# Twenty weight blocks whose low parts come from ScalarE and an adding DMA instead of a VectorE subtraction

## The chip, the core and the metric

The kernel runs on one core of a Trainium2 chip. The core has a matrix engine (TensorE, in the profile PE, with its weight loads as PEld), a vector engine (VectorE, DVE), a scalar engine (ScalarE, ACT), a general engine (GpSimd, POOL) and a queue engine (SyncE, SP) that here issues the DMAs. Each engine works through its own list of instructions in order; semaphores tie the lists together. Sixteen DMA engines move data between DRAM and the on-chip memory SBUF; PSUM holds what TensorE sums.

The metric is the time of one execution in microseconds (us), the median of several. The profile is one execution recorded by the hardware, whose own time stands beside its span.

## The reference

One layer of a bidirectional hybrid encoder on a sequence of 512 tokens, 1024 features, all in float32:

```python
h = rms_norm(x, g[0])
proj = h @ w_in[l]
hy_u, na_qkv, sc_u, gate_pre = jnp.split(proj, splits, axis=-1)
kf = hyena_filters(L, ...)                  # long filters, by a small sine network
y_a = hyena_mixer(hy_u, hy_short_w[l], kf, hy_bias[l])   # two long convolutions, by FFT
y_b = neighbourhood_attention(q, k, v, na_rpb[l])
y_c = short_conv_mixer(b_gate, c_gate, x_in, sc_conv_w[l])
merged = gates[:, :, 0] * (y_a @ w_branch[l, 0]) + ...   # three gated branches
x = x + rms_norm(merged @ w_out[l], g[1])
x = x + rms_norm(memory_cross_attention(...), g[3])
x = x + rms_norm(conv_glu_ffn(...), g[5])
```

The change lies in `h @ w_in`, for 20 of the column blocks of `w_in`: those of the Hyena branch that are not projected earlier (8) and those of the short convolution (12).

## The kernel before

**Split products.** TensorE reads float32 numbers here in a rounded form (F32R). To keep precision, each operand is split into a high part `h`, the rounded value, and a low part `l`, the rest, and `mm3` (L84) adds three products: high by high, high by low, low by high. `split` (L80) makes the parts: `high` (L75) is a ScalarE copy with rounding, `low` (L78) a subtraction, on VectorE unless another engine is named. All these helpers record under one line each, so the profile tells them apart by tile: `wh` and `wl` are high and low part of a weight block, `xh` and `xl` those of the normed input.

**Weight blocks.** A block is 128 partitions by 1024 float32 numbers, 512 KB, and is 128 columns of `w_in`. `block` (L92) takes a `wh` and a `wl` tile (four buffers each) and calls `load_split`: `load_raw` (L108) has SP issue a DMA from DRAM into a `wr` tile (three buffers), ScalarE makes `wh` from `wr`, and VectorE makes `wl` as `wr - wh`. A `wr` buffer is free for the next load when VectorE has read it. A `wh` or `wl` buffer is free when TensorE has done the block that used it, four blocks earlier.

**The projection loop.** `projections` (L308) is a generator over the 20 blocks. It asks for two blocks ahead, then for one more each time before it multiplies one: `project` runs 8 steps of `mm3`, 24 matmuls of 512 columns, into one PSUM bank (`mm`).

**What runs around it.** `go` draws blocks from the generator between the steps of the Hyena branch, so the blocks fill TensorE while the other engines work:

- the filter network: `filter_taps` (twice; tiles `hf`, `ha`, `hb`, `la`, `lb`; GpSimd makes `w` and `w3b`), then `spectra` (tiles `od`, `kt`), whose results go out to DRAM (`kd`) on SP and come back as `kst`;
- the wave matrices: `filter_mats` (`cosh`, `cosl`, `sinh`, `sinl`, the low parts on GpSimd) and `hyena_consts` (`wavef`, `wavee`, `waveo`, loaded by SP as `raw<-in_hy_f`, `_e`, `_o`);
- four convolutions: `conv_in` turns the input with TensorE transposes (L490) and splits it into `sh`, `sl`; `conv_forward` multiplies by `wavef` into `aux` banks, copies two of them by ScalarE into `fly` tiles, combines them on VectorE (L523 to L529), and multiplies by the spectrum into two `ab` tiles (L533 to L537). VectorE finishes one of these with four steps (L543 to L546) and GpSimd the other with the same four. `conv_split` makes `ych`, `ysh` (ScalarE) and `ycl`, `ysl` (VectorE), and `conv_back` multiplies them by `wavee`, `waveo` and gates the result (L570);
- `conv3` on the projected blocks (L322, L323; for most of them ScalarE makes `tap` and GpSimd adds it, L329), and the short convolution (`scg`, `scx`, `sct`, `yc`).

**What sets the order.** A scheduling layer places each instruction in its engine's list ahead of time. What a list holds, and so what a waiting instruction holds up behind it, is fixed when the program is built. After the Hyena branch come the neighbourhood attention, the gates, the cross-attention and the gated MLP, in the same manner.

Of the kernel before, what the change touches and what calls it, by code (L numbers as in the profile page):

```python
# [7 lines left out]
F32R = mybir.dt.float32r  # L8
ACT = mybir.ActivationFunctionType
ALU = mybir.AluOpType  # L10
# [3 lines left out]
P = 128  # L14
# [19 lines left out]
def f(ap):  # L34
    return ap.bitcast(F32)
# [15 lines left out]
class Trunk:  # L51
# [40 lines left out]
    def block(self, src):  # L92

        h = self.base.tile([P, 1024], F32R, tag="wh", bufs=4, name="wh")
        lo = self.base.tile([P, 1024], F32R, tag="wl", bufs=4, name="wl")
        self.load_split(h[:], lo[:], src)
        return h, lo

    def block_parts(self, src):
# [208 lines left out]
    def projections(self, srcs, x):  # L308

        srcs = iter(srcs)  # L310
        ws = [self.block(src) for src in islice(srcs, 2)]
        yield
        while ws:
            ws += [self.block(src) for src in islice(srcs, 1)]
            yield self.project(ws.pop(0), x)

    def conv3(self, out, ps, col, spare=False):
# [1030 lines left out]
```

## Time and profile before

| | |
|---|---|
| median of 3 runs | 1112.19 us (1111.86 to 1113.84) |
| the profiled execution, its own time | 1114.05 us |
| its span, first to last instruction | 1112.3 us |
| mean granted TensorE clock | 0.99 of full speed |
| busy over the span | PE 97%, PEld 81%, DVE 63%, ACT 43%, POOL 9% |
| chain of work that ended last | PE 82%, DVE 9%, DMA 3%, ACT 2%, issue 2%, POOL 1% |

The 1.75 us between the profiled execution's time and its span lie outside the instructions. The busy shares are means over stages that differ. The stage of the 20 blocks lies between about 50 and 240 us, and the views in the prediction are read there: the waits of an engine (who waited for whom), groups of instructions by line and shape, the timeline (start, duration, engine, line, operation; at the end the idle time before it and what ended it), and windows (busy time of each engine in a stretch, with the granted clock). Consecutive matmuls overlap in their records: what a matmul costs TensorE is the step from its start to the next one's.

### The profile page before, as it was taken

How to read it: one execution, taken by the hardware profiler on the slowest of the kernel's cores; microseconds unless marked ns; L12 is line 12 of the kernel's file. 1: busy time of each engine (PE TensorE's matmuls, PEld its weight loads, DVE VectorE, ACT ScalarE, POOL GpSimd, SP SyncE). 2: the span in 40 equal slices, each digit the busy share in tenths (PEclk: the TensorE clock that was granted, in tenths of full speed). 3: DMA queues.
4: the chain of work that ended last, by engine and by line, in shares of the span. 5: the costliest groups of instructions: out<-in, count | busy, mean ns of one | idle time of the engine just before them, and what ended most of it. 6: DMA issues, size and time to landing. Idle time of an engine off the chain costs nothing.

```text
span 1112.3 us, 13562 instructions
## 1 busy us (share of the span) xinstructions
PE 1081.6 (97%) x5232; PEld 903.2 (81%) x5232; DVE 696.5 (63%) x1021; ACT 477.3 (43%) x744; POOL 95.4 (9%) x72
## 2 busy tenths in 40 slices
PE   8889989999999999999999999999999999999997
PEld 6668878887888888888789888889888888888886
DVE  6898799985656564344796546576656565642324
ACT  6553532224557453232565444454444444431221
POOL 0161242221121110000000000000000000000000
PEclk9899999999999999999999999999999999999999
DMA  6354723317423312224526421222222222222212
GB/s 218 105 190 161 246 94 107 103 58 167 125 87 100 112 57 95 95 95 160 200 76 205 156 76 57 76 95 95 95 95 95 95 95 97 102 98 101 95 57 75
DMA packets 43532, 125.48 MB, mean 113 GB/s; under 512 B 5097, under 2 KB 11561, under 8 KB 43468
## 3 DMA queue, kind: packets, MB, share of 16 engines
q1 hardware_dynamic: 43468, 124.62, 33.4%
q8 instruction: 41, 0.67, 0.2%
q14 instruction: 23, 0.19, 0.1%
HBM read 115.16 MB, written 7.34 MB: 110 GB/s over the span
## 4 chain that ended last, share of the span: by engine, by line
PE 82%; DVE 9%; DMA 3%; ACT 2%; issue 2%; POOL 1%; SPq 0%; DVEq 0%; ACTq 0%; POOLq 0%
PE mm L88 25%; PE mm L89 25%; PE mm L90 25%; DVE wl L78 2%; PE aux L725 1%; PE aux L89 1%; PE aux L90 1%; PE aux L88 1%; DMA wr<-in_w_in 1%; PE aux L714 1%; ACT wh L75 1%; PE aux L904 1%; DMA raw<-in_hy_o 1%; POOL w L398 0%; DMA wr<-in_w_out 0%
## 5 line engine op out<-in xcount | busy, mean ns | idle before, releaser
L78 DVE TENSOR_TENSOR wl<-wr,wh 128x1024 fp32r<-128x1024 f32 (+1 forms) x171 | 219.8, 1289 | 254.4 <-ACT wh L75 253.6
L75 ACT ACTIVATE wh<-wr 128x1024 fp32r<-128x1024 f32 (+1 forms) x171 | 180.1, 1054 | 308.1 <-PE mm L89 186.7
L89 PE MATMUL mm<-hl,wh 128*128 128x512 f32 (+1 forms) x448 | 167.5, 374 | 0.0
L88 PE MATMUL mm<-hh,wh 128*128 128x512 f32 (+1 forms) x448 | 167.2, 374 | 0.3 <-ACT hh L75 0.3
L90 PE MATMUL mm<-hh,wl 128*128 128x512 f32 (+1 forms) x448 | 167.4, 374 | 0.0
L88 PE MATMUL mm<-xh,wh 128*128 128x512 f32 x416 | 164.6, 396 | 0.0
L89 PE MATMUL mm<-xl,wh 128*128 128x512 f32 x416 | 163.7, 393 | 0.0
L90 PE MATMUL mm<-xh,wl 128*128 128x512 f32 x416 | 163.6, 393 | 0.0
L89 PEld LDWEIGHTS mm<-hl,wh 128*128 128x128 f32 x448 | 84.4, 188 | 15.0 <-DVE hl L78 0.2
L90 PEld LDWEIGHTS mm<-hh,wl 128*128 128x128 f32 x448 | 84.3, 188 | 15.0
L88 PEld LDWEIGHTS mm<-hh,wh 128*128 128x128 f32 x448 | 84.1, 188 | 15.2 <-ACT hh L75 0.5
L90 PEld LDWEIGHTS mm<-xh,wl 128*128 128x128 f32 x416 | 78.9, 190 | 17.1 <-issue 0.3
L88 PEld LDWEIGHTS mm<-xh,wh 128*128 128x128 f32 x416 | 79.0, 190 | 15.8
L89 PEld LDWEIGHTS mm<-xl,wh 128*128 128x128 f32 x416 | 78.9, 190 | 15.7
L88 PE MATMUL mm<-wh,act 128*128 128x512 f32 x176 | 68.5, 389 | 0.0
L89 PE MATMUL mm<-wl,act 128*128 128x512 f32 x176 | 68.5, 389 | 0.0
L90 PE MATMUL mm<-wh,act 128*128 128x512 f32 x176 | 68.3, 389 | 0.0
L88 PEld LDWEIGHTS mm<-wh,act 128*128 128x128 f32 x176 | 33.0, 188 | 7.1 <-issue 0.3
L75 ACT ACTIVATE act<-u 128x512 fp32r<-128x512 f32 x22 | 13.9, 630 | 57.8 <-DVE u L1024 57.8
L90 PEld LDWEIGHTS mm<-wh,act 128*128 128x128 f32 x176 | 33.0, 188 | 6.9
L89 PEld LDWEIGHTS mm<-wl,act 128*128 128x128 f32 x176 | 33.0, 188 | 6.8
L331 DVE SCALAR_TENSOR_TENSOR u<-mm,cols,u 128x511 f32<-128x511 f32 x44 | 33.0, 751 | 1.5
(342 smaller groups left out, 1938.4 us busy)
## 6 DMA issues: line engine op xcount, KB each, us to landing
wr<-in_w_in SPq DMA_DIRECT2D x55, 512.0 KB, 3.6
wr<-in_ffn_up SPq DMA_DIRECT2D x44, 512.0 KB, 3.5
wr<-in_ffn_down SPq DMA_DIRECT2D x22, 512.0 KB, 3.4
wr<-in_w_branch SPq DMA_DIRECT2D x12, 512.0 KB, 3.4
kd<-kt SPq DMA_DIRECT2D x16, 256.0 KB, 3.9
kst<-kd SPq DMA_DIRECT2D x8, 512.0 KB, 4.9
wr<-in_w_out SPq DMA_DIRECT2D x8, 512.0 KB, 4.3
wr<-in_xa_wk SPq DMA_DIRECT2D x8, 512.0 KB, 3.4
```

Source lines behind the costliest of these rows:

```text
L75: self.nc.scalar.activation(out=out, in_=in_, func=ACT.Copy, bias=0.0, scale=scale)
L78: (eng or self.nc.vector).tensor_tensor(out=out, in0=in_, in1=f(high), op=ALU.subtract)
L88: mm(out, ah, bh, start=first, stop=False)
L89: mm(out, ah, bl, start=False, stop=False)
L90: mm(out, al, bh, start=False, stop=last)
L331: nc.vector.scalar_tensor_tensor(out=out[:, 0 : L - 1], in0=ps[:, 1:L], scalar=self.colvec(w2), in1=out[:, 0 : L - 1], op0=ALU.mult, op1=A ...
L714: nc.tensor.transpose(tr[:, i * P : (i + 1) * P], s[:, i // 2, (i % 2) * P : (i % 2 + 1) * P], self.ident[:])
L725: self.nc.tensor.matmul(po[64 * e : 64 * e + 64, b * P : (b + 1) * P], v[b, j][:, h * 64 : (h + 1) * 64], pt[:, (2 * i + j) * P : (2 * i + ...
L904: self.nc.tensor.transpose(tr[:, k * P : (k + 1) * P], t[:, c : c + P], self.ident[:])
```

## The change

A second function for a weight block, `block_added`, is used by `projections` in place of `block`; all other blocks of the kernel (`block` is also called elsewhere) stay as they were.

```diff
+    def block_added(self, src):
+
+        h = self.base.tile([P, 1024], F32R, tag="wh", bufs=4, name="wh")
+        lo = self.base.tile([P, 1024], F32R, tag="wl", bufs=4, name="wl")
+        self.high(h[:], self.load_raw(src)[:])
+        self.high(lo[:], f(h[:]), -1.0)
+        self.nc.gpsimd.dma_start(out=lo[:], in_=src, accum_op=ALU.add)
+        return h, lo
...
     def projections(self, srcs, x):
 
         srcs = iter(srcs)
-        ws = [self.block(src) for src in islice(srcs, 2)]
+        ws = [self.block_added(src) for src in islice(srcs, 2)]
         yield
         while ws:
-            ws += [self.block(src) for src in islice(srcs, 1)]
+            ws += [self.block_added(src) for src in islice(srcs, 1)]
             yield self.project(ws.pop(0), x)
```

`high(lo, f(h), -1.0)` is a ScalarE copy with scale -1: it writes minus the high part into the `wl` tile. Then GpSimd issues a DMA that reads the weights from DRAM a second time and adds them to what stands in `wl`: the tile ends as `w - h`, as before. Per block one VectorE instruction goes, and one ScalarE instruction and one GpSimd-issued DMA come. In the kernel before, GpSimd issues no DMA at all. The `wr` tile now has one reader, the ScalarE copy that makes `wh`.

The scheduling layer places the new instructions, and moves others. Three places follow; lines of the changed kernel that stand behind the new function carry numbers that are 9 higher.

The first place is GpSimd's list at the start of the stage (`w3` is the tile that the profile calls `w`). Before:

```order
L78 TENSOR_TENSOR w3b_432<-w3_435,w3a_431 128x1024
L78 TENSOR_TENSOR cosl_592<-raw_593,cosh_591 128x512
L78 TENSOR_TENSOR cosl_592<-raw_597,cosh_591 128x512
L78 TENSOR_TENSOR sinl_602<-raw_603,sinh_601 128x512
L78 TENSOR_TENSOR sinl_602<-raw_607,sinh_601 128x512
L398 TENSOR_TENSOR w3_868<-wr_866 128x512 x2
```

The same place of the changed kernel:

```order
L78 TENSOR_TENSOR w3b_432<-w3_435,w3a_431 128x1024
L105 DMA wl_580<-in_w_in 128x1024
L105 DMA wl_587<-in_w_in 128x1024
L407 TENSOR_TENSOR w3_872<-wr_870 128x512 x2
L105 DMA wl_699<-in_w_in 128x1024
L78 TENSOR_TENSOR cosl_594<-raw_595,cosh_593 128x512
L78 TENSOR_TENSOR cosl_594<-raw_599,cosh_593 128x512
L78 TENSOR_TENSOR sinl_604<-raw_605,sinh_603 128x512
L78 TENSOR_TENSOR sinl_604<-raw_609,sinh_603 128x512
L105 DMA wl_776<-in_w_in 128x1024
```

The adding DMAs of the first four blocks stand among the filter work, and the two `w3` additions of the second filter have moved from behind `cosl` and `sinl` to ahead of them.

The second place is GpSimd's list between the first and the second convolution (the four `ab` steps are one convolution's). Before:

```order
L546 TENSOR_TENSOR ab_1291<-ab_1291 128x2x256
L329 TENSOR_TENSOR vx_1335<-vx_1335,tap_1338 128x511
L543 TENSOR_TENSOR ab_1478<-ab_1478 128x2x256
L544 TENSOR_TENSOR ab_1478<-ab_1478 128x2x256
L545 TENSOR_TENSOR ab_1478<-ab_1478 128x2x256
L546 TENSOR_TENSOR ab_1478<-ab_1478 128x2x256
```

And now:

```order
L555 TENSOR_TENSOR ab_1300<-ab_1300 128x2x256
L338 TENSOR_TENSOR vx_1345<-vx_1345,tap_1348 128x511
L105 DMA wl_1505<-in_w_in 128x1024
L105 DMA wl_1591<-in_w_in 128x1024
L105 DMA wl_1649<-in_w_in 128x1024
L552 TENSOR_TENSOR ab_1490<-ab_1490 128x2x256
L553 TENSOR_TENSOR ab_1490<-ab_1490 128x2x256
L554 TENSOR_TENSOR ab_1490<-ab_1490 128x2x256
L555 TENSOR_TENSOR ab_1490<-ab_1490 128x2x256
```

Three adding DMAs, those of the 13th to 15th block, stand ahead of the second convolution's `ab` steps. Three stand ahead of the third convolution's, and two ahead of the fourth's.

The third place is ScalarE's list around the `fly` copies of the first convolution. Before:

```order
L75 ACTIVATE waveoh<-raw 128x1024
L322 ACTIVATE vx<-mm,cols 128x512
L75 ACTIVATE wh<-wr 128x1024
L75 ACTIVATE tap<-mm,cols 128x511
L75 ACTIVATE fly<-aux 128x512 x2
L75 ACTIVATE wh<-wr 128x1024
```

And now:

```order
L75 ACTIVATE waveoh<-raw 128x1024
L75 ACTIVATE wh<-wr 128x1024
L331 ACTIVATE vx<-mm,cols 128x512
L75 ACTIVATE fly<-aux 128x512
L75 ACTIVATE wl<-wh 128x1024
L75 ACTIVATE tap<-mm,cols 128x511
L75 ACTIVATE fly<-aux 128x512
L75 ACTIVATE wh<-wr 128x1024
```

A `wl<-wh` copy now stands between the two `fly` copies; in the second half of each `spectra`, `wl<-wh` and `tap` have come ahead of `od<-aux` in the same way.

On VectorE the 20 `wl` rows are gone; what is left has nearly its old order.

## The prediction

> **What bounds the kernel now.** Over the whole span TensorE is busy 97% and the chain that ended last lies 82% on it, so a gain can only come from TensorE's idle time, and a loss from new idle time there. The change touches the stage between about 50 and 240 us, so the windows come first.
>
> ```profile
> core 0: us, PE busy (x) PEld busy (x) DVE busy (x) ACT busy (x) POOL busy (x), PEclk, DMA share, GB/s
> 60.00:80.00 20.00, 16.99 (x68) 13.52 (x68) 19.22 (x23) 10.53 (x16) 15.50 (x7) 0.91 0.51 163
> 140.00:160.00 20.00, 16.53 (x77) 13.55 (x76) 19.93 (x20) 7.91 (x10) 11.09 (x7) 1.00 0.24 81
> 160.00:180.00 20.00, 19.90 (x114) 18.07 (x115) 19.95 (x23) 2.86 (x4) 3.31 (x2) 0.91 0.31 105
> 180.00:200.00 20.00, 18.93 (x108) 16.30 (x107) 18.24 (x21) 8.34 (x11) 3.30 (x3) 1.00 0.31 104
> ```
>
> VectorE is full (19.2 to 19.95 of 20 us) just where TensorE has holes, ScalarE and GpSimd are not. The second view says what ended the holes, from 50 to 230 us (total, times, longest), with SP's queue at the end.
>
> ```profile
> PE aux L89 <- DVE sl L78: 5.1, 2, 3.6
> PE aux L412 <- DVE hf L415: 3.6, 2, 3.0
> PE aux L490 <- DVE vx L570: 1.4, 2, 1.1
> PE aux L89 <- DVE la L78: 1.0, 1, 1.0
> SPq L110 <- DVE wl L78: 102.3, 20, 23.5
> ```
>
> TensorE waited 5.1 + 3.6 + 1.4 + 1.0 = 11.1 us, every time for VectorE, and never for a `wl` itself. In two of the windows the clock fell to 0.91 besides, which costs 0.09 x 20 = 1.8 us each; both dips come right after a wait of 3 us or more. So 11.1 + 3.6 = **14.7 us** is all that can be won.
>
> **What goes and what comes.** The groups of this stage:
>
> ```profile
> L78 DVE TENSOR_TENSOR wl<-wr,wh 128x1024 fp32r<-128x1024 f32 x20 | 29.8, 1502 | 1.0 <-ACT wh L75 1.0
> L75 ACT ACTIVATE wh<-wr 128x1024 fp32r<-128x1024 f32 x21 | 22.2, 1057 | 48.8 <-PE mm L89 42.2 <-PE mm L90 4.4 <-DMA wr<-in_w_in 2.2
> L545 POOL TENSOR_TENSOR ab<-ab 128x512 f32<-128x512 f32 x3 | 4.9, 1620 | 0.2
> L398 POOL TENSOR_TENSOR w<-wr 128x512 f32<-128x512 f32 x2 | 5.5, 2783 | 1.0 <-DMA wr<-in_hy_w 1.0
> ```
>
> Removed: 20 x 1.50 = 30 us of VectorE. Added: 20 copies of the same shape as `wh`, 20 x 1.06 = 21 us of ScalarE, which has room except where it stands on a chain (below). Added: 20 adding DMAs, of which this trace shows none. Two prices of theirs are unknown. GpSimd's time to issue one lies between SP's issue of a load of the same size (0.80 us, row below) and GpSimd's slowest tensor instruction (2.78); an issue being nearer to an issue, I take 0.8. For its landing, and its share of the DMA engines, the wave loads are the nearest rows:
>
> ```profile
> 128.59 0.80 SPq L472 DMA_DIRECT2D raw<-in_hy_e  x1
> 129.44 0.76 SPq L472 DMA_DIRECT2D raw<-in_hy_o  x1
> 134.48 1.06 ACT L75 ACTIVATE waveeh<-raw 128x1024 fp32r<-128x1024 f32 x1 [0.16 <-DMA raw<-in_hy_e]
> 135.77 1.06 ACT L75 ACTIVATE waveoh<-raw 128x1024 fp32r<-128x1024 f32 x1 [0.22 <-DMA raw<-in_hy_o]
> wr<-in_w_in SPq DMA_DIRECT2D x55, 512.0 KB, 3.6
> ```
>
> A 512 KB load lands 3.6 us after its issue, in traffic 6.3 (129.44 to 135.75), and two in flight land 1.3 us apart. An adding DMA reads the weights and the tile, so I take twice: 7.2 us to land (bounds 3.6 and 12.6), 2.6 us of all engines.
>
> Does TensorE wait for it? The shortest lead is the first block's:
>
> ```profile
> 49.86 1.06 ACT L75 ACTIVATE wh<-wr 128x1024 fp32r<-128x1024 f32 x1 [2.89 <-PE mm L90]
> 67.75 0.39 PE L88 MATMUL mm<-xh,wh 128*128 128x512 f32 x1
> 215.97 1.06 ACT L75 ACTIVATE wh<-wr 128x1024 fp32r<-128x1024 f32 x1 [1.71 <-PE mm L89]
> ```
>
> 17.9 us from the start of `wh` to the first use, less two copies: 15.8 us for issue and landing, against 8.0 taken and 15.4 at the upper bounds. The four buffers hide it; it costs nothing while it stays below. The 20th `wh` starts at 215.97, so a block comes every (215.97 - 49.86) / 19 = 8.7 us. SP's 102.3 us behind `wl` also end earlier, since `wr` is now free after `wh`; I count nothing for it, as TensorE waited for no load here.
>
> **Term 1, the filter taps.**
>
> ```profile
> 55.38 1.05 ACT L75 ACTIVATE wh<-wr 128x1024 fp32r<-128x1024 f32 x1
> 62.35 5.30 POOL L78 TENSOR_TENSOR cosl<-raw,cosh 128x512 fp32r<-128x512 f32 x2 [22.83 <-DVE vx L331]
> 63.59 1.21 DVE L78 TENSOR_TENSOR wl<-wr,wh 128x1024 fp32r<-128x1024 f32 x1
> 66.42 4.52 DVE L78 TENSOR_TENSOR wl<-wr,wh 128x1024 fp32r<-128x1024 f32 x2
> 71.60 0.50 PE L412 MATMUL aux<-w3a,h2s 128*128 128x512 f32 x1 [3.01 <-DVE hf L415]
> 80.41 0.39 PE L90 MATMUL aux<-ha,cosl 128*128 128x512 f32 x1
> ```
>
> Three `wl` (1.21 + 4.52 = 5.7 us) stand ahead of the first `hf` that TensorE waits for. Without them `hf` starts when its `aux` bank is full, and the 3.0 us and the dip behind it (1.8) go: **-4.8**. Next is GpSimd, where `w3` and one DMA have moved ahead of `cosl`: `hy_w` can load when the second `wh` is made, at 55.38 + 1.05 = 56.4, and lands 3.6 later; `w` 5.5, the DMA 0.8 and `cosl` 5.3 then end at 71.6, and TensorE would want `cosl` at 80.4 - 4.8 = 75.6. It fits by 4.0 us. The 1.0 for `la` I leave to such waits.
>
> **Term 2, the first convolution.**
>
> ```profile
> 138.38 3.10 DVE L78 TENSOR_TENSOR wl<-wr,wh 128x1024 fp32r<-128x1024 f32 x1 [0.20 <-ACT wh L75]
> 138.87 1.08 ACT L75 ACTIVATE fly<-aux 128x512 f32<-128x512 f32 x2
> 141.40 0.68 DVE L526 TENSOR_TENSOR fly<-aux,fly 128x512 f32<-128x512 f32 x1
> 143.91 1.22 DVE L528 TENSOR_TENSOR fly<-fly 128x1024 f32<-128x1024 f32 x1
> 156.56 2.29 DVE L78 TENSOR_TENSOR wl<-wr,wh 128x1024 fp32r<-128x1024 f32 x1
> 160.10 0.38 PE L89 MATMUL aux<-sl,wavefh 128*128 128x256 f32 x1 [3.57 <-DVE sl L78]
> ```
>
> The 3.10 us `wl` holds `fly` back to 141.40, but little of it is won: `fly` on ScalarE, ended at 139.95, now has a `wl<-wh` between its copies (+1.06), and one stands ahead of `od` at the head of the chain that leads to the wave loads (+1.06). The second copy ends at 142.1, two VectorE steps of 0.6 follow, and L528 starts at 143.3 instead of 143.91: 0.6 earlier. The 2.29 us at 156.56 go whole. That makes 2.9. Against it the wave loads share the engines with adding DMAs, one in 8.7 us, so at most one of 2.6 us falls into their 6.3: between 0 and 2.6 later, I take 1.3. Of the wait, 3.57 - 2.9 + 1.3 = 2.0 is left; it falls by 1.6, and a wait of 2 us should bring no dip (the 1.1 us wait for `vx` brought none: the window 180:200 has clock 1.00): **-3.4**.
>
> **Term 3, the other convolutions.**
>
> ```profile
> 186.78 1.22 DVE L78 TENSOR_TENSOR wl<-wr,wh 128x1024 fp32r<-128x1024 f32 x1
> 190.85 1.21 DVE L78 TENSOR_TENSOR wl<-wr,wh 128x1024 fp32r<-128x1024 f32 x1
> 197.55 1.06 ACT L75 ACTIVATE wh<-wr 128x1024 fp32r<-128x1024 f32 x1 [5.32 <-PE mm L89]
> 203.10 1.61 POOL L543 TENSOR_TENSOR ab<-ab 128x512 f32<-128x512 f32 x1 [19.73 <-DVE ab L537]
> ```
>
> Three `wl` of 1.2 us stand in each round (of this one the first and the last). The waits there are 5.1 - 3.6 = 1.5 for `sl` and 1.4 for `vx`, 2.9 together. But ahead of `ab` L543 GpSimd now has three adding DMAs. The last waits for a `wh` that TensorE releases (197.55) and a copy: 197.55 + 2.1 + 0.8 = 200.5, while `ab`, some 2.2 us earlier than 203.10, would be ready at 200.9. It fits by 0.4 us only; what is queued behind that DMA is the `ab` chain, for which `ysh`, `ysl` and then `sl` wait. I give half away: **-1.5**.
>
> **The sum:** -4.8 - 3.4 - 1.5 = -9.7 us. The profiled execution, 1114.05 us (span 1112.3 and 1.75 around it), becomes 1104.35. It is 1.86 above the median of the runs, 1112.19, which becomes **1102.5 us**. Behind 240 us nothing is changed, and TensorE passes the gain on.
>
> **A rule that speaks against it.** GpSimd and VectorE do hinder each other here: `wl` took VectorE 3.10 and 2.29 us (138.38, 156.56) in and just ahead of the window in which GpSimd was busy 11.09 us, and 1.21 in the rounds behind.
>
> ```profile
> 137.30 1.05 ACT L75 ACTIVATE wh<-wr 128x1024 fp32r<-128x1024 f32 x1
> 163.95 0.63 PE L88 MATMUL mm<-xh,wh 128*128 128x512 f32 x1
> ```
>
> The rival drawn from this: issues are held until VectorE pauses. It was full from 140 to 180 (19.93 and 19.95 of 20). The block with `wh` at 137.30 is multiplied from 163.95; its issue after 180 and landing 7.2 us later would make TensorE wait some 23 us: 1112 + 23 - 10 = 1125 us. Against it: GpSimd's own 11.09 us fell into that stretch. The Trainium skill, "SBUF — State Buffer", section "Who interferes with whom", says that a DMA which VectorE seems to stall is one whose descriptors GpSimd makes, starved of port time; by that rule the sum would be the rival's. The same section infers that a two-input VectorE sum or difference, as here, takes only the read side, which making descriptors doesn't need; by that the sum stays. No row here shows a DMA of this kind.
>
> **The rivals and their chances.**
> - Forecast: VectorE leaves the path, TensorE is nearly closed up; 1097.5 (all 14.7 won) to 1107: **0.58**.
> - New waits eat most: issues of 2.8 us, not 0.8, make the last DMA of a round end 1.6 us after `ab` is ready, and terms 2 and 3 vanish: 4.8 won, 1107.4: **0.12**. The margin of 0.4 us speaks for it, GpSimd's idle 19.73 us ahead of `ab` against, in which the other two issues fit.
> - The edit does what it says, but the end stays: the wave loads hang on SP and ScalarE, not on TensorE, and come the full 2.6 us later; what term 1 wins in front TensorE then waits at 160.10, and the rounds behind gain nothing: 1112 within 2.2: **0.12**. ScalarE's longer chain to `fly` speaks for it, the 2.29 us `wl` behind it against.
> - Slower: adding DMAs go one after another, each longer than the 8.7 us in which a block comes. At 10 us the 19 steps last 19 x 1.3 = 25 us longer: 1137. It decides from 8.7 us in series; the wave loads, 1.3 us apart, make it 2.6 for two reads, though 12.6 us to land is in the bounds: **0.12**.
> - Slower, issues held by VectorE: 1125: **0.06**.
>
> Within 0.2% (2.2 us) of before is what a measurement of this kernel can't tell from no change. So faster 0.58 + 0.12 = 0.70, same 0.12, slower 0.18. The range 1097 to 1114 leaves out the slower cases and little else.
>
> **What would show it.** Right: the 3.0 us wait at 71.6 and the one at 160 gone or under 2 us, clock 1.00 in both windows, `mm` on `wl` never waiting for a DMA, and `ab` L543 released by VectorE, not by an issue. Wrong: TensorE waiting on DMA `wl`, adding DMAs that land more than 15 us after their issue, GpSimd issues above 2 us or a gap ahead of `ab`, or the wave loads landing later than 7.6 us.

## The result, and the profile after

| | before | after |
|---|---|---|
| median of the runs | 1111.46 us (9 runs, 1108.24 to 1113.84) | 1104.1 us (9 runs, 1102.1 to 1108.37) |
| ratio, with its 95% interval | | 0.994 (0.9924 to 0.9956) |
| the profiled execution, its own time | 1114.05 us | 1103.86 us |
| its span | 1112.3 us | 1102.1 us |

The change makes the kernel 7.4 us faster by the medians, against 9.7 forecast. The time lies in the range, and the sign is right. But the three terms did not share the gain as forecast.

The page of the kernel after (DMA queues with packets, MB and share of 16 engines; the chain that ended last; the adding DMAs with KB each and us to landing):

```profile
q0 software_dynamic: 2880, 10.49, 5.4%
PE 88%; DVE 5%; DMA 3%; issue 2%; ACT 1%; POOL 0%; SPq 0%; DVEq 0%; ACTq 0%
wl<-in_w_in POOLq DMA_DIRECT2D x20, 512.0 KB, 5.9
```

The chain lies 88% on TensorE, where it lay 82% before, and VectorE's share has fallen from 9% to 5%. One adding DMA takes 0.054 x 1102 / 20 = 3.0 us of all engines and lands in 5.9 us. I had taken 2.6 and 7.2. The groups of the stage, 50 to 230 us (busy, mean ns | idle before):

```profile
L105 POOL DMA_DIRECT2D wl<-in_w_in x20 | 17.8, 888 | 97.5 <-ACT wl L75 97.5
L75 ACT ACTIVATE wl<-wh 128x1024 fp32r<-128x1024 f32 x20 | 21.1, 1055 | 0.2
```

An issue takes GpSimd 0.89 us and a copy takes ScalarE 1.06, as taken. The windows of the stage (the last three numbers of a row are the granted clock, the DMA share and GB/s), then the waits from 50 to 230 us:

```profile
60.00:80.00 20.00, 16.40 (x65) 12.97 (x64) 15.47 (x20) 13.13 (x21) 13.61 (x9) 0.91 0.99 280
140.00:160.00 20.00, 18.68 (x97) 15.68 (x97) 19.61 (x19) 10.97 (x15) 10.91 (x9) 1.00 0.71 192
160.00:180.00 20.00, 18.42 (x107) 16.08 (x106) 17.69 (x20) 6.25 (x8) 8.34 (x6) 1.00 0.72 181
```

```profile
PE aux L421 <- DVE hf L424: 3.6, 1, 3.6
PE aux L499 <- DVE vx L579: 1.6, 1, 1.6
PE aux L89 <- DVE sl L78: 1.3, 1, 1.3
```

Of 11.1 us of waits 6.5 are left. The dip of the clock in 160 to 180 is gone. The one in 60 to 80 is still there, and so is the wait ahead of it at the filter taps. The timeline of TensorE in the kernel after shows where they stand:

```profile
40.87 0.47 PE L88 MATMUL mm<-wh,eh 128*128 128x512 f32 x1 [3.68 <-DVE scaled L290]
...
72.21 0.50 PE L421 MATMUL aux<-w3a,h2s 128*128 128x512 f32 x1 [3.60 <-DVE hf L424]
...
155.73 0.39 PE L89 MATMUL aux<-sl,wavefh 128*128 128x256 f32 x1 [1.32 <-DVE sl L78]
...
177.02 1.35 PE L499 MATMUL aux<-ident,vx 128*128 128x128 f32 x8 [1.58 <-DVE vx L579]
...
263.89 0.36 PE L704 MATMUL aux<-kb,qa 128*128 128x256 f32 x1 [0.99 <-DMA kb<-ka]
```

The same view of the kernel before, at the first and last of these places and at two waits that are gone or have moved:

```profile
42.67 0.77 PE L88 MATMUL mm<-wh,eh 128*128 128x512 f32 x1 [3.62 <-DVE scaled L281]
...
182.90 0.75 PE L490 MATMUL aux<-ident,vx 128*128 128x128 f32 x4 [1.06 <-DVE vx L570]
...
217.76 0.38 PE L89 MATMUL aux<-sl,wavefh 128*128 128x256 f32 x1 [1.50 <-DVE sl L78]
...
272.84 0.36 PE L695 MATMUL aux<-kb,qa 128*128 128x256 f32 x1 [1.93 <-DMA kb<-ka]
```

The profiled executions differ by 10.2 us, the medians by 7.4. The first row of each shows where 1.8 us of that come from: after is ahead by so much at 40 us, before any changed instruction. In a second profile of the same changed kernel that row stands elsewhere:

```profile
42.45 0.69 PE L88 MATMUL mm<-wh,eh 128*128 128x512 f32 x1 [3.69 <-DVE scaled L290]
```

So the 1.8 us are an execution's, not the change's: the granted clock in the first 20 us was 0.91 in before and in this second profile, and 1.00 in the first profile of after, and 0.09 x 20 = 1.8. From that row to the first `kb,qa` (all of the changed stage and some 30 us behind it) before takes 272.84 - 42.67 = 230.2 us and after 263.89 - 40.87 = 223.0. That is **-7.2 us**, close to the medians. I call this distance the stage length, and the table of experiments uses it. The last 1.2 us of the 10.2 lie behind the `kb,qa` row: in 260 to 280 us before has a granted clock of 0.91, behind its wait of 1.93 us for `kb`, and after has 1.00.

**What the wait at the taps is now.** The kernel after, VectorE and then GpSimd:

```profile
65.00 1.89 DVE L424 TENSOR_TENSOR hf<-aux,dec 128x512 f32<-128x512 f32 x3 [2.23 <-PE aux L422]
66.80 4.76 DVE L429 TENSOR_TENSOR hf<-hf 1x512 f32<-1x512 f32 x1
71.48 0.67 DVE L424 TENSOR_TENSOR hf<-aux,dec 128x512 f32<-128x512 f32 x1
```

```profile
65.11 0.87 POOL L105 DMA_DIRECT2D wl<-in_w_in  x1
65.72 2.85 POOL L78 TENSOR_TENSOR cosl<-raw,cosh 128x512 fp32r<-128x512 f32 x2
68.22 2.78 POOL L78 TENSOR_TENSOR sinl<-raw,sinh 128x512 fp32r<-128x512 f32 x2
```

The three `wl` are gone and the first `hf` starts when its bank is full, as forecast. Then a step on one row of 512 numbers, which took 0.67 us before, takes 4.76. It ends 0.6 us after GpSimd's four subtractions (71.56 against 71.00). Behind it stands the fourth `hf`, for which TensorE waits. The Trainium skill, "SBUF — State Buffer", section "Who interferes with whom", says that a VectorE instruction with two inputs in SBUF contends with a GpSimd instruction that reads SBUF; its section "Summary: rules for kernel authors" says that of such a pair the second to issue is blocked until the first finishes. The trace agrees in kind: the `hf` products, with one input from PSUM (`aux`), ran in 0.6 us each beside `cosl`, and the one-row sum, with both in SBUF, did not. But it was kept out until four instructions had ended, not one.

### The profile page after: what moved, and what is told of

Read it like the earlier page. It is cut to its first block, busy times and chain, and to the rows that moved or that the text cites. A ratio compares the mean times of both kernels' runs of the same rounds, so it can differ in the third digit from the quotient of the medians.

```text
span 1102.1 us, 13606 instructions
## 1 busy us (share of the span) xinstructions
PE 1077.2 (98%) x5232; PEld 899.8 (82%) x5232; DVE 670.5 (61%) x1001; ACT 495.4 (45%) x764; POOL 104.2 (9%) x92
## 4 chain that ended last, share of the span: by engine, by line
PE 88%; DVE 5%; DMA 3%; issue 2%; ACT 1%; POOL 0%; SPq 0%; DVEq 0%; ACTq 0%
PE mm L90 26%; PE mm L88 26%; PE mm L89 26%; PE aux L89 2%; PE aux L90 2%; PE aux L88 2%; PE aux L734 1%; DMA wr<-in_w_out 1%; DMA wr<-in_w_in 1%; PE aux L723 1%; DVE wl L78 1%; PE aux L913 1%; ACT wh L75 1%; DMA dec<-in_decay 1%; DVE hf L429 0%
## 5 line engine op out<-in xcount | busy, mean ns | idle before, releaser
L78 DVE TENSOR_TENSOR wl<-wr,wh 128x1024 fp32r<-128x1024 f32 (+1 forms) x151 | 191.4, 1269 | 251.2 <-ACT wh L75 250.5
L1030 ACT ACTIVATE u<-u 128x512 f32<-128x512 f32 x22 | 13.9, 633 | 45.4 <-DVE u L340 45.4
```

The source lines that it names most:

```text
L78: (eng or self.nc.vector).tensor_tensor(out=out, in0=in_, in1=f(high), op=ALU.subtract)
L1030: nc.scalar.activation(out=u[:], in_=u[:], func=ACT.Gelu_apprx_tanh)
```

## The experiments

All ratios are against the kernel before, run on the same chip. "Stage" is the change of the stage length in the profiled execution.

| kernel | median, us | ratio (95%) | stage, us | longest wait at the taps, us |
|---|---|---|---|---|
| after | 1104.1 | 0.994 (0.9924 to 0.9956) | -7.2 | 3.6 |
| last 12 blocks only | 1106.91 | 0.9951 (0.9934 to 0.9967) | -5.9 | 3.0 |
| first 8 blocks only | 1112.02 | 0.9997 (0.9979 to 1.0014) | 0.0 | 3.6 |
| without the DMA | 1099.76 | 0.9882 (0.9859 to 0.9905) | -12.0 | 0.2 |
| without low parts | 1102.93 | 0.992 (0.9894 to 0.9946) | -8.8 | 2.3 |
| DMA of 16 columns | 1103.49 | 0.9917 (0.9901 to 0.9933) | -8.2 | 4.3 |
| one-row step later | 1105.78 | 0.9939 (0.9921 to 0.9957) | -6.6 | 4.3 |
| `cosl`, `sinl` on VectorE | 1107.86 | 0.996 (0.9946 to 0.9975) | -3.8 | 0.5 |
| third issue behind `sinl` | 1103.03 | 0.9927 (0.9914 to 0.9939) | -8.8 | 1.3 |
| and tenth behind `waveol` | 1108.32 | 0.9959 (0.9941 to 0.9977) | -5.3 | 0.2 |
| after, once more | 1106.87 | 0.9949 (0.9932 to 0.9966) | -7.6 | 3.6 |
| each DMA twice | 1142.85 | 1.0271 (1.0252 to 1.0289) | +29.5 | none |
| subtractions on GpSimd | 1128.52 | 1.0143 (1.0128 to 1.0157) | +18.2 | 3.4 |

Before stands at 3.0 us in the last column. The two series of after differ by 2.8 us in their medians, on different chips, so kernels are compared by their ratios.

### Which blocks the gain comes from

```diff
-        ws = [self.block_added(src) for src in islice(srcs, 2)]
+        made = iter(range(20))
+
+        def one(src):
+            return (self.block_added if next(made) >= 8 else self.block)(src)
+
+        ws = [one(src) for src in islice(srcs, 2)]
...
-            ws += [self.block_added(src) for src in islice(srcs, 1)]
+            ws += [one(src) for src in islice(srcs, 1)]
```

> Only the last 12 of the 20 blocks are made the new way, the first 8 by VectorE as before. Theory (the gain is made from the first convolution on): 1104 to 1105.5 us, the waits for sl as in the changed kernel. Rival (the gain goes by the number of subtractions, 12 of 20 of 7.4 us): 1107 us.

The second kernel has `< 8` for `>= 8`.

> Only the first 8 of the 20 blocks are made the new way. Theory: nothing is won at the filter taps, 1110 to 1112 us, and the waits of 3.6 us for sl and at the taps both stay. Rival (by number, 8 of 20): 1108.5 us.

The last twelve blocks give 1 - 0.9951 = 0.49%, or 5.4 us, and the first eight 0.03%, nothing that can be measured. Together that is 0.52%, and the whole change gave 0.60% (0.44 to 0.76), so the parts add up. The late kernel's 1106.91 us is the 1107 of its rival, by number of blocks, and decides nothing alone; the early kernel does, at 1112.02 where that rival had 1108.5. The gain is in the convolutions. The waits for `sl`, late kernel and then early kernel:

```profile
PE aux L89 <- DVE sl L78: 1.8, 1, 1.8
```

```profile
PE aux L89 <- DVE sl L78: 5.0, 3, 2.4
```

The early kernel keeps the 5 us of the convolutions that before had, and gets the held one-row step at the taps (4.73 us there, and a wait of 3.6) in exchange for its `wl`.

### The cost of the adding DMA, and of the low parts at all

```diff
-        self.nc.gpsimd.dma_start(out=lo[:], in_=src, accum_op=ALU.add)
```

> The adding DMA is left out: wl holds minus the high part, so the output is not the reference's. Theory (the gain is VectorE's relief, and adding DMAs, GpSimd issues and ScalarE copies cost nothing on TensorE's path): 1104 us within 2, as the changed kernel, and the 3.6 us wait for hf at the filter taps stays. Rival (the DMAs' traffic takes part of the gain back; dec landed in 6.0 us instead of 3.0): 1101 us or less, dec landing in about 3 us, the wait at the taps down to 1 us or less.

The rival is right. The ratio is 0.9882, against 0.994 for after: the adding DMA, its issues included, costs 0.58% or 6.4 us by the ratios (4.3 by the medians, 4.9 by the stage). GpSimd, VectorE, and the row that ends the stage length, in this kernel:

```profile
63.37 3.44 POOL L78 TENSOR_TENSOR cosl<-raw,cosh 128x512 fp32r<-128x512 f32 x2
66.77 3.00 POOL L78 TENSOR_TENSOR sinl<-raw,sinh 128x512 fp32r<-128x512 f32 x2
```

```profile
67.37 1.23 DVE L428 TENSOR_TENSOR hf<-hf 1x512 f32<-1x512 f32 x1
```

```profile
258.86 0.42 PE L703 MATMUL aux<-kb,qa 128*128 128x256 f32 x1 [2.78 <-DMA kb<-ka]
```

With no issue ahead of `cosl`, GpSimd needs 1.7 us for each of its first two subtractions instead of 1.4, VectorE gets its turn between them, and the one-row step takes 1.23 us. The rows show one more difference. Here `sinl` starts as `cosl` ends (63.37 + 3.44 = 66.81 against 66.77); in after it started 0.35 us before `cosl` ended (65.72 + 2.85 = 68.57 against 68.22). The wait at the taps is 0.2 us. Not all that is won in front arrives: at `kb,qa` TensorE now waits 2.78 us for a DMA, where after waits 0.99.

```diff
         h = self.base.tile([P, 1024], F32R, tag="wh", bufs=4, name="wh")
-        lo = self.base.tile([P, 1024], F32R, tag="wl", bufs=4, name="wl")
         self.high(h[:], self.load_raw(src)[:])
-        self.high(lo[:], f(h[:]), -1.0)
-        self.nc.gpsimd.dma_start(out=lo[:], in_=src, accum_op=ALU.add)
-        return h, lo
+        return h, h
```

> The 20 blocks get no low part at all (the high part stands in for it; same matmuls, other numbers): no VectorE subtraction, no ScalarE copy, no DMA. Theory: 1104 us within 2, since TensorE waits for almost nothing in the convolutions any more. Rival (copies on ScalarE ahead of od and fly, and the DMAs, cost something): 1099 to 1101 us; the 1.3 us wait for sl and the 1.6 us wait for vx at the first convolutions gone.

With no low part to make the ratio is 0.992 and the time in the theory's range; of the two waits that the rival named, the one for `sl` is gone and the one for `vx` is not (1.4 us). It is slower than the kernel that makes the copies. Fewer instructions gave another order: the first `mm<-xh` came at 72.64 us instead of 67.53, and TensorE waited 2.3 us at the taps. So this is no floor, and I draw only this from it: below some point the order at the taps counts for more than the work of the low parts.

### Traffic, or the issue

```diff
-        self.nc.gpsimd.dma_start(out=lo[:], in_=src, accum_op=ALU.add)
+        self.nc.gpsimd.dma_start(out=lo[:, 0:16], in_=src[:, 0:16], accum_op=ALU.add)
```

> The adding DMA takes 16 of the 1024 columns only (the other columns of the low parts stay at minus the high part, so the output isn't the reference's). Every instruction stands where it stood, and GpSimd still issues 20 DMAs at about 0.9 us each; only the traffic goes. THEORY (traffic: what the DMA costs is the share of the 16 engines that it takes, by which `dec` lands in 6.0 us instead of 3.0 and the loads of the convolutions come later): the time falls to that of the kernel without the DMA, 1099 to 1101 us, `dec` lands in 3 to 4 us, and the wait at the filter taps falls under 1 us. RIVAL (the cost is GpSimd's: its issues and the place they give to `w`, `cosl` and `sinl`, beside which the one-row step of the taps is held for 4.8 us): the time stays at 1103 to 1105 us, the one-row step still takes over 4 us and TensorE still waits 3 us or more at the taps.

Neither theory alone: 0.9917 lies between 0.994 and 0.9882. `dec` lands in 3.1 us (6.0 in after, 3.0 before), and TensorE waits for no `sl` any more, so the traffic did cost something in the first convolution (its rows stand under term 2 below). But the hold at the taps needs no traffic. GpSimd and VectorE:

```profile
63.45 0.87 POOL L105 DMA_DIRECT2D wl<-in_w_in  x1
64.06 2.83 POOL L78 TENSOR_TENSOR cosl<-raw,cosh 128x512 fp32r<-128x512 f32 x2
```

```profile
62.27 1.78 DVE L340 SCALAR_TENSOR_TENSOR vx<-scaled,cols,vx 128x511 f32<-128x511 f32 x1
63.98 5.89 DVE L340 SCALAR_TENSOR_TENSOR vx<-tap,cols,vx 128x511 f32<-128x511 f32 x1
```

These rows show two manners in one kernel. Beside `w`, ahead of the issue, `vx` steps and GpSimd take turns (1.78 us instead of 0.74). Behind the issue GpSimd runs all four subtractions through, and the `vx` step that meets them takes 5.89 us. It is another step than in after, since GpSimd is 1.7 us earlier here; which step is held hangs on the moment, and TensorE waits 4.3 us.

### Three ways out of the hold

The one-row steps behind the next two `hf`:

```diff
+            parts.append(part)
             if not t:
-
-                s = part[0][0:1, :]
-                nc.vector.tensor_tensor(out=s, in0=s, in1=part[1][0:1, :], op=ALU.add)
+                continue
+            if t == 1:
+                first, s = parts[0], parts[0][0][0:1, :]
+                nc.vector.tensor_tensor(out=s, in0=s, in1=first[1][0:1, :], op=ALU.add)
...
+            for tt in ((0, 1) if t == 1 else (t,)):
+                for n, s in zip("ab", parts[tt]):
```

> In the filter taps the two one-row steps on `hf` (and the splits of the first quarter) come behind the four products `hf` of the first two quarters instead of behind the first two. THEORY (the wait at the taps is there because VectorE's one-row step, held 4.8 us beside GpSimd's `cosl` and `sinl`, stands ahead of the `hf` for which TensorE waits): the wait falls from 3.6 to under 1 us and the dip of the clock behind it goes, 1099 to 1101.5 us. RIVAL (whatever VectorE does at that place is held just as long, or the `dec` that lands in 6 us is late next): TensorE waits 2.5 us or more in the taps still, and the time stays at 1103 to 1105 us.

The rival is right. VectorE:

```profile
65.83 5.89 DVE L340 SCALAR_TENSOR_TENSOR vx<-tap,cols,vx 128x511 f32<-128x511 f32 x1
```

GpSimd starts `cosl` at 65.91 in this kernel, and the hold falls on the last `vx` ahead of the `hf`. Moving VectorE's instruction away did not help, because another with two inputs in SBUF stood in its place.

GpSimd's subtractions given to VectorE:

```diff
-                self.split(h[:, c], lo[:, c], raw[:], nc.gpsimd)
+                self.split(h[:, c], lo[:, c], raw[:])
```

> The low parts of the two filter matrices (`cosl`, `sinl`: four subtractions of 128x512) are made by VectorE instead of GpSimd. THEORY (GpSimd's subtractions hold the one-row step): with them gone the one-row step takes 0.7 to 1.3 us; against that VectorE has 4 x 0.67 = 2.7 us more ahead of it, so the wait at the taps falls from 3.6 to 1 to 2 us, 1100 to 1103 us. RIVAL (the step is held by the traffic or the issues of the adding DMAs): it takes over 3 us still, the wait grows by the 2.7 us to about 6 us, 1106 to 1108 us.

VectorE, and TensorE's longest wait:

```profile
70.61 0.67 DVE L429 TENSOR_TENSOR hf<-hf 1x512 f32<-1x512 f32 x1
```

```profile
80.71 0.76 PE L88 MATMUL aux<-ha,cosh 128*128 128x512 f32 x1 [4.22 <-DVE hf L424]
```

With the DMAs and their issues left in, the step is back at 0.67 us: GpSimd's subtractions hold it, not the DMA. The waits at the taps are 0.4 and 0.5 us. But the last four `hf` now wait for a late `dec` load, TensorE waits 4.2 us for them, and the kernel is slower than after. I had not foreseen that wait; the time lies in the rival's range, though its reason is refuted by the 0.67.

One issue moved behind `sinl`, by a factor that GpSimd can only make then:

```diff
+        self.minus = pool.tile([P, 1], F32, name="minus")
+        nc.gpsimd.tensor_scalar(out=self.minus[:], in0=f(lo[:, 1023:1024]), scalar1=0.0, scalar2=-1.0, op0=ALU.mult, op1=ALU.add)
...
-        self.high(lo[:], f(h[:]), -1.0)
+        self.high(lo[:], f(h[:]), scale)
...
+        scale = self.minus[:, 0:1]
         while ws:
-            ws += [self.block_added(src) for src in islice(srcs, 1)]
+            ws += [self.block_added(src, scale) for src in islice(srcs, 1)]
+            scale = -1.0
```

> All 20 low parts as in the changed kernel; only the third block's copy takes its factor -1 from a column that GpSimd computes from `sinl`, so that this block's adding DMA stands behind `cosl` and `sinl` in GpSimd's list instead of ahead of them. THEORY (GpSimd's four subtractions keep VectorE out for their whole 5.3 us when a DMA issue stands directly ahead of them, and take turns with VectorE when none does, as in the kernel without the DMA): `cosl` and `sinl` take 1.6 to 1.8 us each, no VectorE step beside them takes over 2.5 us, TensorE waits under 1 us at the filter taps and the clock stays at 1.00 there; the time is that of the kernel without the DMA plus what its traffic costs in the first convolution (2.3 us by the traces), 1100 to 1102.5 us. RIVAL (which of the two it is hangs on the moment at which they meet, or on the traffic, not on the issue ahead): one VectorE step is still held for over 4 us, TensorE waits 3 us or more at the taps, 1103 to 1105 us.

GpSimd, VectorE, and two windows of this kernel:

```profile
64.30 3.44 POOL L78 TENSOR_TENSOR cosl<-raw,cosh 128x512 fp32r<-128x512 f32 x2
67.96 2.72 POOL L78 TENSOR_TENSOR sinl<-raw,sinh 128x512 fp32r<-128x512 f32 x2 [0.23 <-ACT sinh L75]
```

```profile
70.00 1.22 DVE L433 TENSOR_TENSOR hf<-hf 1x512 f32<-1x512 f32 x1
```

```profile
40.00:60.00 20.00, 19.01 (x71) 15.53 (x72) 17.00 (x29) 13.69 (x19) 1.88 (x2) 0.82 0.46 129
60.00:80.00 20.00, 18.23 (x76) 13.51 (x75) 20.00 (x23) 14.95 (x22) 13.90 (x10) 1.00 0.94 259
```

The engines take turns again, no VectorE step beside the four subtractions takes more than 1.8 us, the wait falls from 3.6 to 1.3 (under 1 was expected), and the clock in 60 to 80 is 1.00. So the place of one issue in GpSimd's list decides the hold. The moment does not: `cosl` started at 64.04 us in the kernel without low parts, where the engines took turns, and at 64.06 with the DMA of 16 columns, where VectorE was held, with `vx` steps on VectorE in both. The time is less clear. At 1103.03 us it lies just outside the theory's range, and 0.9927 stands against 0.994 and 0.9949 for the two series of after, with intervals that overlap. In this profile the dip at 40 to 60, ahead of the change, was deeper than in after (0.82 against 0.91, 1.8 us). So this version beats before; that it beats after too is only likely.

One issue more, the tenth block's, moved behind the wave loads:

```diff
+        self.minus2 = pool.tile([P, 1], F32, name="minus2")
+        nc.gpsimd.tensor_scalar(out=self.minus2[:], in0=f(lo[:, 1023:1024]), scalar1=0.0, scalar2=-1.0, op0=ALU.mult, op1=ALU.add)
...
+            n += 1
-            scale = -1.0
+            scale = self.minus2[:, 0:1] if n == 9 else -1.0
```

> As the kernel with the third adding DMA behind `sinl`; the tenth block's copy besides takes its -1 from a column that GpSimd computes from `waveol`, so that its adding DMA is issued behind the three wave loads instead of beside them. THEORY (the 1.3 us that TensorE waits for `sl` in the first convolution come from that DMA's traffic, which lets the wave loads land later): the wait for `sl` falls under 0.4 us, 1101 to 1102.5 us. RIVAL (the copy and the issue that come later delay the `fly` and `ab` chains behind them, or the block itself): a wait of 1 us or more for `sl`, `sh` or a `wl` is there still, 1103 to 1105.5 us.

The wait for `sl` is 1.3 us still, as the rival has it, but the time of 1108.32 us lies above both ranges. The waits, and the tenth block's copy on ScalarE:

```profile
PE aux L88 <- ACT sh L75: 1.9, 1, 1.9
PE aux L89 <- DVE la L78: 1.7, 1, 1.7
PE aux L89 <- DVE sl L78: 1.3, 1, 1.3
```

```profile
140.17 1.16 ACT L75 ACTIVATE wl<-wh,minus 128x1024 fp32r<-128x1024 f32 x1 [1.89 <-POOL minus L491]
```

The copy stands between the two `fly` copies and waits 1.89 us for GpSimd, so the chain to `sh` and `sl` runs later, and TensorE has a new wait of 1.9 us for `sh`. The wait for `la`, at 80 us, stands far ahead of the tenth block. The moved DMA was not what delays the wave loads: `raw<-in_hy_e` landed 6.3 us after its issue with it and without it. The load ahead of that, `raw<-in_hy_f`, is late already. From its issue to the copy `wavefh` that waits for it there are 6.9 us in after and 6.4 in these two kernels, 5.5 in before and 4.8 with the DMA of 16 columns, and another adding DMA is issued 1.4 us behind it. That one may be the cause; no run moved it.

The kernel after ran beside this one:

> The changed kernel once more, on the chip of the run beside it. THEORY (VectorE held at the taps costs what the trace shows, and moving one or two issues wins it back): 1103.5 to 1105 us, 1 us or more above the kernel run with it. RIVAL (no difference): the two medians within 0.5 us of each other.

It was 1.4 us faster than the kernel with two issues moved, so neither expectation fits. It repeats the held step (4.74 us) and the wait (3.6).

### Two prices from above

```diff
         self.nc.gpsimd.dma_start(out=lo[:], in_=src, accum_op=ALU.add)
+        self.nc.gpsimd.dma_start(out=lo[:], in_=src, accum_op=ALU.add)
```

> Each adding DMA is issued twice (the weights are added twice, so the output isn't the reference's): twice the traffic, 40 issues. THEORY (traffic): the 4.3 us that the kernel without the DMA gains are paid once more, 1107 to 1110 us, each DMA lands later (8 to 12 us), `dec` in 8 us or more; TensorE still never waits for a `wl`, since both end within the 15.8 us lead. RIVAL (the cost is a single clash at the taps, not the traffic): landings double just as well, but the time stays at 1103 to 1105.5 us.

Both were far off, and the run does not double the traffic alone. The group of the second issue, from 50 to 300 us:

```profile
L106 POOL DMA_DIRECT2D wl<-in_w_in x20 | 17.5, 875 | 120.0 <-DMA wl<-in_w_in 96.6 <-PE aux L90 7.3 <-PE aux L423 6.6
```

The second DMA adds to what the first has written, so GpSimd stands still 120 us, nearly all of it until first DMAs have landed, with its list queued behind. What the run shows is the price of adding DMAs in series on an engine that also computes: 30 us more than before, and some 37 more than after.

```diff
-        self.high(h[:], self.load_raw(src)[:])
-        self.high(lo[:], f(h[:]), -1.0)
-        self.nc.gpsimd.dma_start(out=lo[:], in_=src, accum_op=ALU.add)
+        self.load_split(h[:], lo[:], src, self.nc.gpsimd)
```

> The 20 low parts are subtracted by GpSimd (no copy on ScalarE, no DMA). THEORY (a two-input subtraction on GpSimd keeps VectorE out as long as it lasts): 20 x 2.4 us = 48 us of GpSimd (`w3b` of the same shape took 2.4), VectorE steps beside them take 2 to 3 us instead of 0.7, and the last subtraction of a round ends 1.5 us later than an issue would, so `ab` and `sl` come later; 1104 to 1109 us. RIVAL (VectorE has room for that since it does 30 us less, and the traffic of the adding DMA is gone): as without the DMA, 1099 to 1102 us.

The group in the stage:

```profile
L78 POOL TENSOR_TENSOR wl<-wr,wh 128x1024 fp32r<-128x1024 f32 x18 | 47.6, 2645 | 68.5 <-ACT wh L75 48.4 <-DVE vx L330 12.9 <-PE aux L420 7.1
```

At 2.6 us each, the same subtractions on GpSimd cost 16 us more than on VectorE, and by the ratios some 23 more than with the DMA. The mechanism is the first theory's (a pair of `la` takes VectorE 5.56 us beside them), but the time is 20 us above its range.

## Why the prediction was right, and where it was not

The time and the sign came as forecast; of the three terms one failed, one came out by two errors that cancel, and one held. That the sum landed 1.6 us from the forecast is in part luck.

**Term 1, the filter taps (-4.8): failed.** The step that fell is "without them `hf` starts when its `aux` bank is full, and the 3.0 us and the dip behind it go". The first half held, the second did not: the wait is 3.60 us, the dip is there. Working GpSimd's margin for `cosl` (4.0 us) I took its time from the kernel before and asked only whether it ends in time, not whom it shuts out meanwhile. The 5.3 us for two `cosl` in before were turns with VectorE; with a DMA issue ahead of them it was 2.85, at VectorE's cost. The runs show it from three sides: without the subtractions on GpSimd the step takes 0.67 us, with the issue elsewhere 1.22, with a DMA that moves almost nothing the hold stays. And the first eight blocks alone give no gain. What the stage did win in front are the small waits for `la` (1.0 in before, none in after), which I had left uncounted.

**Term 2, the first convolution (-3.4): right in its total, with two errors that cancel.** The wait fell from 3.57 to 1.32 us, where 2.0 was forecast, and the dip went: 2.25 + 1.8 = 4.05. The 2.29 us `wl` went whole. What lies ahead of it is read from the first `sl` matmul of the round. Before:

```profile
136.14 0.28 PE L89 MATMUL aux<-sl,wavefh 128*128 128x256 f32 x1
```

After, and then the kernel whose DMA adds 16 columns:

```profile
133.64 1.06 ACT L75 ACTIVATE waveeh<-raw 128x1024 fp32r<-128x1024 f32 x1 [2.16 <-DMA raw<-in_hy_e]
133.85 0.28 PE L89 MATMUL aux<-sl,wavefh 128*128 128x256 f32 x1
141.73 1.23 DVE L537 TENSOR_TENSOR fly<-fly 128x1024 f32<-128x1024 f32 x1
```

```profile
132.25 1.06 ACT L75 ACTIVATE waveeh<-raw 128x1024 fp32r<-128x1024 f32 x1 [0.54 <-DMA raw<-in_hy_e]
134.09 0.28 PE L89 MATMUL aux<-sl,wavefh 128*128 128x256 f32 x1
140.16 1.22 DVE L537 TENSOR_TENSOR fly<-fly 128x1024 f32<-128x1024 f32 x1
```

The copy `waveeh`, which waits for its load, starts 1.7 us ahead of that matmul in before (136.14 - 134.48), 0.2 in after and 1.8 with little traffic. So the adding DMAs brought this load 1.5 us later, near the 1.3 taken; it took only 0.2 us longer itself (6.1 for 5.9), but was issued 1.2 us later by the same measure. L528, L537 in after, starts 7.8 us behind that matmul in before, 7.9 in after and 6.1 with little traffic. So the `fly` steps win 1.7 us where 0.6 was forecast, and the traffic takes 1.8 from them. What is left is the 2.29 us `wl`, close to the 2.25 by which the wait fell. One more reason failed: that a wait of 2 us brings no dip. In before the wait of 1.93 us for `kb` was followed by a granted clock of 0.66 in the next 5 us. The wait fell below that, so the 1.8 us came all the same.

**Term 3, the other convolutions (-1.5): right.** The waits of 2.9 us became one of 1.58, so -1.3; the `sl` waits went and a `vx` wait stayed. The margin that I gave half away for was larger than 0.4 us. GpSimd in the round of the kernel after that I had used:

```profile
194.46 0.86 POOL L105 DMA_DIRECT2D wl<-in_w_in  x1 [6.53 <-ACT wl L75]
196.55 1.60 POOL L552 TENSOR_TENSOR ab<-ab 128x512 f32<-128x512 f32 x1 [1.22 <-DVE ab L546]
```

The issue was done 1.2 us before VectorE released `ab`. Terms 2 and 3 together, -5.4, are what the last twelve blocks give alone (5.4), though by waits that differ in part: that kernel waits 1.8 us for `sl` and 1.8 for `la`.

**The sum.** 4.05 + 1.3 is 5.4 of the 7.2; the 1.0 for `la` and a wait of 0.57 us for `hf` at 107 in before, gone too, make it 7.0; 0.6 is lost at the taps (3.60 for 3.01). The other 0.8 I put to the wait for `kb` (1.93, now 0.99), behind the changed stage. So a term of 4.8 fell away, which leaves 4.9 of the forecast, and the other 2.3 of the 7.2 came from what I had left out or priced too low.

**What was to show it, and the rivals.** The wait at 160 is under 2 us and the clock behind it 1.00; the wait and the dip at the taps, which were to go, stayed. TensorE never waited for a `wl`, and issues took 0.89 us with VectorE full beside them (19.61 of 20 in 140 to 160). The rival drawn from issues that VectorE holds did not come; the hold went the other way, from GpSimd to VectorE. Landing in 5.9 us against a block every 8.7, the DMAs never stood in series; the doubled kernel cost 30 us, near my 25 for that rival, but by another way, since there GpSimd's list stood still. The 16-column run puts some 2.6 us (0.994 less 0.9917) on the traffic, and what is left up to 0.9882, 3.9 us, on the issues and the hold; the interval of the 16-column run overlaps both its neighbours', and its hold is longer than in after (5.89 us against 4.76), so the split is rough.

## What to carry over

When work leaves an engine, the instructions left on it move to other neighbours: check each two-input VectorE step on the new path against what GpSimd will be doing at that moment, not only against GpSimd's deadline. An accumulating DMA can take a subtraction off VectorE at a ScalarE copy of 1.06 us, 0.89 us of issue and 3.0 us of DMA time per 512 KB, but its place in GpSimd's list is part of its price. A time of one engine read beside another (`cosl` at 2.65 us each) may be a time of both, and changes when either moves.

## What was not expected of the hardware

Two manners of sharing between VectorE and GpSimd appear with the same instructions. In turns: up to 1.7 us for a GpSimd subtraction and 1.77 for a VectorE step (without the DMA, without low parts, and with issues moved; in before and with the last twelve blocks too, where `cosl` takes 2.65 us each beside longer `wl` steps). In one piece: GpSimd starts a subtraction every 1.3 us, four in a row, and the VectorE step beside them takes 4.7 to 5.9 us (after in both series, the first eight blocks, the one-row step later, the DMA of 16 columns). In every profile with the second manner a DMA issue stands directly ahead of the four; in none with the first. The doubled kernel, with two issues directly ahead, shows the second over three subtractions (two `lb` steps take 4.00 us beside them instead of 1.27). Why an issue decides it, no run shows. But the records differ in one more thing, in all of these profiles: behind an issue each of the next subtractions starts 0.3 us or more before the one ahead of it has ended, and without one at most 0.05. If that is so on the engine, VectorE finds no gap between them; GpSimd's spans are rough, and no run tests this.

The clock dips hang on the length of TensorE's waits. In these kernels, from 50 to 300 us, every wait of 1.2 to 1.8 us that had none close ahead of it was followed by 1.00 in the next 5 us. Waits of 1.9 us and more were followed by 0.50 to 0.75 (0.66 after 1.93 and after 3.6, 0.50 to 0.55 after 4.2 to 4.3), with three exceptions that were followed by 1.00 (2.23 and 2.89 us for `kb`, 2.65 in the doubled kernel). At 0.66 that is 0.34 x 5 = 1.7 us, an estimate of what a wait costs besides itself.
